# The partition sums of the late adaLN vectors issued one gate block later

## The chip, the cores and the metric

The kernel runs on one core of a Trainium2 chip. The metric is device time in microseconds (us) of one execution, lower is better. The core has five engines with instruction queues of their own: TensorE (PE, its weight loads are shown as PEld), VectorE (DVE), ScalarE (ACT), GpSimd (POOL) and SyncE (SP), which here only issues DMAs. Each queue is worked off in the order in which the program put it.

## What is computed

A decoder layer for one sequence of 1024 rows and 1024 columns. A conditioning vector `c` gives six vectors of 1024 numbers each; two of them scale and shift the input before the first half, two do so before the second, and two are gates on what the halves add:

```python
mod = jax.nn.silu(c) @ w_ada[l] + b_ada[l]
shift1, scale1, gate1, shift2, scale2, gate2 = [m[:, None, :] for m in jnp.split(mod, 6, axis=-1)]
h = layer_norm(x) * (1.0 + scale1) + shift1
z = h @ w_in[l]                       # columns for attention, S5 and two merge gates
...
mix = (jax.nn.sigmoid(g_a) * y_a + jax.nn.sigmoid(g_b) * y_b) @ w_o[l]
x = layer_norm(alpha * x + gate1 * mix) * ln1_g[l] + ln1_b[l]
h2 = layer_norm(x) * (1.0 + scale2) + shift2
...
x = layer_norm(alpha * x + gate2 * ff) * ln2_g[l] + ln2_b[l]
```

`y_a` is attention with three branches over `z`, `y_b` a linear recurrence (S5) with a gated linear unit, and `ff` a gated MLP with a convolution of width 3.

## The kernel before, in words

Products are made in pieces: an operand is split into a high and a low part, and three matmuls (lines 131 to 133, `mm3`) of 128x512 make one product. A product of 128 output columns with all 1024 rows (`gemmT`) is 48 such matmuls, in two halves of 24.

After `h` is made, sixteen **gate blocks** `z_gate(0)` to `z_gate(15)` compute the merge gates, 128 columns each; below they are called z0 to z15. They are followed by **jobs**: `r0` and `r1` (the raw keys and values for the compressed branch, tile `kc`), then keys, queries and the rest. z0 to r1 are 18 blocks whose order on TensorE, VectorE, ScalarE and GpSimd is that of the program text (`manual_schedule`); later parts are ordered by a scheduler.

One gate block does this, in the order of the text: fetch its split weights and split those of the next block (ScalarE line 112 makes the high part `wh`, VectorE or GpSimd line 113 the low part `wl`; both have two buffers, so the split waits until TensorE has finished the block before); pass the last block's product through a tanh (`z_out`, line 825); two **late steps** in z4 to z15; a piece of the S5 work (`s5_block`), with a second piece between the two halves of the product; and the product itself, tile `zm`.

The S5 work goes in four groups. On TensorE a group is `s5pk`, `s5pu` (lines 644, 650), then `s5pw` (669, transposes of `s5W`, which GpSimd makes), then `s5pb` (690), and at last `s5py` (748, 750), which needs the tile `s5X` that VectorE finishes at lines 731 and 732 after products and scans (704 to 725).

The late steps build the four vectors scale2 (v = 4), shift2 (3), gate1 (2) and gate2 (5). Each needs eight steps `late(v, k)`: a slab of 128x1024 of `w_ada` is multiplied by one column of silu(c) and added to an accumulator `acc` on VectorE (line 270 for the first, 272 for the others). Two steps go with each gate block, so v = 4 is complete in z7, v = 3 in z11 and v = 2 in z15. The eighth step is followed at once by the **sum over the 128 partitions** on TensorE:

- for v = 4 and 3, `ada_cols` (line 263): eight matmuls of a 128x128 piece of `acc` with a column of ones into the tile `adac` (the profile shows 16 records), and VectorE adds the bias (line 264, tile `mod`);
- for v = 2 and 5, two matmuls with the ones as the weights (line 801, tile `grow`, four records), VectorE adds them to a row `brow` that SP loaded (lines 798 and 802), and SP stores the row in DRAM (line 803, `gr_d`).

v = 5 has its eight steps one by one in the eight turns of the loop over `d` after attention. The weight slabs arrive in a ring `wr` of three buffers, loaded by SP (line 89).

Of the kernel before, what the change touches and what calls it, by code (L numbers as in the profile page):

```python
# [33 lines left out]
def kernel(  # L34
# [13 lines left out]
    def ap(t, off, *dims):  # L48
        return bass.AP(tensor=t.tensor, offset=t.offset + off, ap=[list(d) for d in dims])
# [4 lines left out]
    def Bt(shape, dt=F32, name="b"):  # L54
        return sp.tile(shape, dt, name=name, tag="B", bufs=20)
# [7 lines left out]
    def ps(shape=(P, 512), name="ps"):  # L63
        return pp.tile(list(shape), F32, name=name, tag="ps", bufs=4)
# [195 lines left out]
    def ada_cols(v, acc, k0=0, nk=KD):  # L260
        p = ps(name="adac")
        for k in range(nk):
            TE.matmul(p[:, k:k + 1], acc[:, P * k:P * k + P], ones[:, 0:1], start=True, stop=True)
        V.scalar_tensor_tensor(mod[:, MOD[v], k0:k0 + nk], p[:, 0:nk], 1.0 if v in (1, 4) else 0.0,
                               modb[:, 8 + 8 * v + k0:8 + 8 * v + k0 + nk], op0=OP.add, op1=OP.add)
# [495 lines left out]
    def s5_block(budget):  # L761

        debt[0] = max(debt[0] - budget, -budget)
        while debt[0] < 0:
            t = next(s5, 0)
            if t == 0:
                break
            if t is None:
                debt[0] = 0.0
                break  # L770
            debt[0] += t
        block[0] += 1
# [13 lines left out]
    def late(v, k, hold={}):  # L786
        if k == 0:
            hold[v] = Bt([P, 1024], name="acc")
        ada_acc(hold[v], late_i[v, k], k)
        if k < KD - 1:  # L790
            return
        acc = hold.pop(v)
        if v in (3, 4):
            ada_cols(v, acc)
            return
        gi = 0 if v == 2 else 1
        br = Bt([1, 1024], name="brow")
        SP.dma_start(br, ap(b_ada, v * D, [0, 1], [1, D]))
        for h in range(2):
            p = ps(name="grow")  # L800
            TE.matmul(p[0:1], ones[:, 0:1], acc[:, 512 * h:512 * h + 512], start=True, stop=True)
            V.tensor_add(br[:, 512 * h:512 * h + 512], br[:, 512 * h:512 * h + 512], p[0:1])
        SP.dma_start(gr_d[gi:gi + 1], br)

    sgs = {}

    def z_gate(m):
        wh, wl = W.get(zm_i[m])
        if m:
            z_out(m - 1)  # L810
        late_steps("z", m)
        s5_block(S5_US)
        sgs[m] = mm("zm")
        gemmT(sgs[m], wh, wl, hH, hL, KD)
# [3 lines left out]
    def late_steps(kind, n):  # L818
        for _ in range(n_late(kind, n)):
            late(*lateada[late_n[0]])  # L820
            late_n[0] += 1

    def z_out(m):
        sg = Bt([P, 1024], name="sg")
        A.activation(sg, sgs.pop(m), AF.Tanh, scale=0.5)
        A.dma_start(zm_d[m], sg)
# [149 lines left out]
    with tc.manual_schedule(engines={V.engine, A.engine, G.engine, TE.engine}):  # L976
        for kind, n in ORDER[:N_HAND]:
            if kind != "z":
                if n == 0 and kind == "r":
                    z_out(15)  # L980
                s5_block(S5_US)
            jobs[kind](n)
            if kind != "z":
                late_steps(kind, n)
    assert next(s5, 0) == 0
    S5 = uc = None
    for kind, n in ORDER[N_HAND:-1]:
# [225 lines left out]
    def load_sg(d):  # L1213
        if d < KD:
            ga, gb = Bt([P, 1024], name="ga"), Bt([P, 1024], name="gb")
            SP.dma_start(ga, zm_d[d])
            SP.dma_start(gb, zm_d[8 + d])
            sgs[d] = (ga, gb)
# [12 lines left out]
    for d in range(KD):  # L1231
        ga, gb = sgs.pop(d)
        wa = W.get(p3_i[d][0])
        pz = mm("z1")
        gemmT(pz, wa[0][:, 1], wa[1][:, 1], lambda k: yT[k][0], lambda k: yT[k][1], 4)
        pa = mm("ya")
        gemmT(pa, wa[0][:, 0], wa[1][:, 0], lambda k: oT[k][0], lambda k: oT[k][1], 4)
        wb = W.get(p3_i[d][1])
        late(5, d)
        load_sg(d + 1)  # L1240
        V.scalar_tensor_tensor(ga, ga, 1.0, pa, op0=OP.add, op1=OP.mult)
        s2 = Ct([P, 1024], name="s2")
        for h in range(2):
            c0 = slice(512 * h, 512 * h + 512)
            pg = ps(name="zg2")
            for k in range(4):
                mm3(pg, wb[0][:, k], wb[1][:, k], yT[k][0][:, c0], yT[k][1][:, c0], k == 0, k == 3)
            A.activation(s2[:, c0], pg, AF.Tanh, scale=0.5)
            V.scalar_tensor_tensor(s2[:, c0], s2[:, c0], 1.0, pz[:, c0], op0=OP.add, op1=OP.mult)
            V.scalar_tensor_tensor(s2[:, c0], gb[:, c0], 1.0, s2[:, c0], op0=OP.add, op1=OP.mult)  # L1250
            V.scalar_tensor_tensor(mixF[h][:, d], s2[:, c0], 0.5, ga[:, c0], op0=OP.mult, op1=OP.add)
        if 2 <= d < 6:
            wo.append(W.get(wo_i[d - 2]))
        if d == 5:
            split_mix(0, (0,))
# [538 lines left out]
```

## Time and profile before

| what | us |
|---|---|
| median of 3 runs | 1666.48 |
| lowest and highest of them | 1665.79, 1666.56 |
| the profiled execution, its own time | 1662.42 |
| its span, first to last instruction | 1660.7 |
| TensorE busy in the span | 1559.5 (94%) |
| VectorE busy | 1246.9 (75%) |
| ScalarE busy | 687.6 (41%) |
| GpSimd busy | 664.9 (40%) |

The span is 1.72 us shorter than the execution's own time, which has the start and the end around it. The profiled execution is 4.06 us under the median of the runs. A busy share says how long an engine had instructions in work, not who held up whom. For that there are the chain that ended last, the list of waits, and the timeline with the idle time in front of each instruction in square brackets and, behind the arrow, what ended it. [...]

### The profile page before, as it was taken

The numbers are of one execution on the slowest core, as the hardware profiler recorded it, in microseconds if no ns is written. First come the engines' busy times: TensorE is split into PE (matmuls) and PEld (weight loads), VectorE is DVE, ScalarE is ACT, GpSimd is POOL, SyncE is SP. The second block draws the span as 40 slices with busy tenths as digits, with TensorE's granted clock in tenths as the row PEclk, the third lists the DMA queues.
The fourth block names the chain that finished last, engine by engine and source line by source line (L and its number), as shares of the span: only waits on it lengthen the run. The fifth ranks groups of instructions, "written<-read, shape, count | busy, mean of one in ns | idle before, by whom it ended". The sixth has DMA issues, their size and how long they took to land.

```text
span 1660.7 us, 21550 instructions
## 1 busy us (share of the span) xinstructions
PE 1559.5 (94%) x7707; PEld 1304.5 (79%) x7707; DVE 1246.9 (75%) x2302; ACT 687.6 (41%) x1309; POOL 664.9 (40%) x559
## 2 busy tenths in 40 slices
PE   7999899899999999999999677999999998899996
PEld 4888788688989999778787455888888886688885
DVE  8698687555399999756686878888888887855448
ACT  4324323234399999512313633444444343311101
POOL 5345434000066566222425014555555555532006
PEclk8999899999999999999999798999999999999998
DMA  9334555422200010454511112222222237422102
GB/s 342 78 90 123 166 173 168 131 77 81 60 20 1 14 39 2 143 170 146 174 55 64 63 29 86 87 91 77 76 77 89 77 110 267 168 102 102 38 11 92
DMA packets 150129, 164.36 MB, mean 99 GB/s; under 512 B 20633, under 2 KB 123777, under 8 KB 150021
## 3 DMA queue, kind: packets, MB, share of 16 engines
q1 hardware_dynamic: 146357, 151.74, 28.7%
q10 hardware_dynamic: 3664, 11.24, 2.0%
q8 instruction: 61, 1.00, 0.3%
q14 instruction: 47, 0.39, 0.1%
HBM read 132.04 MB, written 30.91 MB: 98 GB/s over the span
## 4 chain that ended last, share of the span: by engine, by line
PE 73%; DVE 16%; ACT 5%; issue 3%; DMA 2%; SPq 0%; POOL 0%; DVEq 0%; ACTq 0%
PE up L1462 4%; PE up L1463 4%; PE up L1464 4%; PE dn L1610 4%; PE dn L1612 4%; PE dn L1611 4%; PE oacc L1096 3%; PE zm L131 3%; PE zm L132 3%; PE zm L133 3%; PE upX L1462 2%; PE pT L1107 2%; PE upX L1463 2%; PE upX L1464 2%; ACT Pm L1066 2%
## 5 line engine op out<-in xcount | busy, mean ns | idle before, releaser
L1070 POOL TENSOR_SCALAR Pm<-Pm,gate,fc 128x64 f32<-128x64 f32 (+4 forms) x192 | 124.3, 664 | 56.8 <-DVE fc L1068 56.2
L112 ACT ACTIVATE wh<-wr 128x1024 fp32r<-128x1024 f32 (+3 forms) x59 | 57.7, 978 | 184.6 <-PE zm L132 64.0
L1610 PE MATMUL dn<-dnh,fh 128*128 128x512 f32 x320 | 124.6, 389 | 0.9 <-DVE facc L1759 0.9
L1759 DVE SCALAR_TENSOR_TENSOR facc<-facc,dn 128x512 f32<-128x512 f32 x96 | 64.5, 682 | 80.2 <-PE dn L1612 80.0
L1611 PE MATMUL dn<-dnl,fh 128*128 128x512 f32 x320 | 124.5, 389 | 0.0
L1612 PE MATMUL dn<-dnh,fl 128*128 128x512 f32 x320 | 124.5, 389 | 0.0
L1066 ACT ACTIVATE Pm<-Pm,ng 128x64 f32<-128x64 f32 (+6 forms) x192 | 114.6, 602 | 6.4 <-DVE ng L1047 5.0
L111 POOL TENSOR_TENSOR wr<-wr,g2b 128x1024 f32<-128x1024 f32 x22 | 65.1, 2973 | 118.1 <-DMA wr<-in_w_down_dram 101.9
L1530 POOL TENSOR_TENSOR cv<-cv 128x1024 f32<-128x1024 f32 x22 | 62.1, 2825 | 118.1 <-ACT cv L1529 118.1
L1111 DVE TENSOR_TENSOR Pt<-pT,Pt 128x512 fp32r<-128x512 f32 (+1 forms) x160 | 100.6, 643 | 9.7 <-ACT Pt L1110 8.2
L1096 PE MATMUL oacc<-Pt,Vs 128*128 128x256 f32 x528 | 102.7, 304 | 0.9 <-DVE Pt L1111 0.4
L131 PE MATMUL zm<-hTh,wh 128*128 128x512 f32 x256 | 101.5, 397 | 0.4 <-ACT uc L582 0.4
L133 PE MATMUL zm<-hTh,wl 128*128 128x512 f32 x256 | 100.0, 391 | 1.5 <-DVE wl L113 1.5
L1391 POOL TENSOR_TENSOR ul<-wr,uh 128x512 fp32r<-128x512 f32 x40 | 69.6, 1761 | 76.1 <-ACT uh L1390 76.1
L132 PE MATMUL zm<-hTl,wh 128*128 128x512 f32 x256 | 100.1, 391 | 0.0
L1107 PE MATMUL pT<-ident,Pm 128*128 128x128 f32 x592 | 91.3, 273 | 1.9 <-DVE yl L1170 1.0
L1110 ACT ACTIVATE Pt<-pT 128x512 fp32r<-128x512 f32 (+1 forms) x160 | 87.4, 560 | 13.0 <-PE pT L1107 11.8
L113 DVE TENSOR_TENSOR wl<-wr,wh 128x1024 fp32r<-128x1024 f32 (+2 forms) x40 | 54.5, 1363 | 45.4 <-ACT wh L112 45.3
L113 POOL TENSOR_TENSOR wl<-wr,wh 128x1024 fp32r<-128x1024 f32 (+1 forms) x19 | 40.8, 2148 | 114.2 <-ACT wh L112 112.2
L1462 PE MATMUL up<-h2b,uh 128*128 128x512 f32 (+1 forms) x184 | 72.2, 392 | 14.4 <-DVE bias L1475 11.6
L1489 DVE SCALAR_TENSOR_TENSOR cv<-up,cw,cv 128x511 f32<-128x511 f32 x88 | 65.6, 745 | 20.7 <-ACT cv L1484 19.1
L1096 PEld LDWEIGHTS oacc<-Pt,Vs 128*128 128x128 f32 x528 | 75.5, 190 | 5.4 <-DVE Pt L1111 3.1
(487 smaller groups left out, 4817.6 us busy)
## 6 DMA issues: line engine op xcount, KB each, us to landing
wr<-in_w_up_dram SPq DMA_DIRECT2D x44, 512.0 KB, 4.7
wr<-in_w_in_dram SPq DMA_DIRECT2D x32, 512.0 KB, 5.9
wr<-in_w_ada_dram SPq DMA_DIRECT2D x32, 512.0 KB, 4.4
ff_d<-cv SPq DMA_DIRECT2D x22, 512.0 KB, 2.6
wr<-in_w_down_dram SPq DMA_DIRECT2D x22, 512.0 KB, 3.5
fl<-ff_d SPq DMA_DIRECT2D x22, 512.0 KB, 6.6
ar<-in_w_ada_dram SPq DMA_DIRECT2D x16, 512.0 KB, 9.8
zm_d<-sg ACTq DMA_DIRECT2D x16, 512.0 KB, 3.8
```

Of the source, the lines that this page charges most:

```text
L131: TE.matmul(po, wh, rh, start=start, stop=False, skip_group_check=skip)
L132: TE.matmul(po, wh, rl, start=False, stop=False, skip_group_check=skip)
L133: TE.matmul(po, wl, rh, start=False, stop=stop, skip_group_check=skip)
L1066: A.activation(Pm[ii][:, c0:c0 + n], Pm[ii][:, c0:c0 + n], AF.Exp, bias=ng[:, ii, br:br + 1], scale=-1.0, accum_out=dn[:, ii, br:br + 1])
L1070: G.tensor_scalar(Pm[ii][:, c0:c0 + n], Pm[ii][:, c0:c0 + n], gate[:, i, 3 * h + br:3 * h + br + 1], fc[:, ii, br:br + 1], op0=OP.mult, op ...
L1096: TE.matmul(acc[:, a0:a0 + 256], vt, ptile[:, hl, 256 * w:256 * w + 256], start=(first and n == 1), stop=(last and n == nmm), skip_group_c ...
L1107: TE.transpose(p[:, o:o + P], Pm[e][:, c0:c0 + P], ident)
L1111: V.tensor_sub(pt[:, 1, 0:wt], p[:, 0:wt], pt[:, 0, 0:wt].bitcast(F32))
L1462: TE.matmul(po, wh[:, q], h, start=(q == 0 and j not in (3, 4, 7)), stop=False, skip_group_check=True)
L1610: TE.matmul(p, ff[0][:, c0], wd[0][:, s], start=(e == 0), stop=False)
L1611: TE.matmul(p, ff[0][:, c0], wd[1][:, s], start=False, stop=False)
L1612: TE.matmul(p, ff[1][:, c0], wd[0][:, s], start=False, stop=(e == len(fs) - 1))
```

## The change

The eighth step now only puts the finished accumulator on a list (`late_sum`). A new function `late_sums` makes the sums of what is on the list, with the same instructions as before. It is called in three places: in each gate block after `z_out` and before that block's own late steps; in r0 after `z_out(15)`; and in the loop over `d`, in its last turn, right after the step, which is where the sum of v = 5 was before. A call of `late_steps` for jobs that have no late steps is dropped.

```diff
         ada_acc(hold[v], late_i[v, k], k)
         if k < KD - 1:
             return
-        acc = hold.pop(v)
-        if v in (3, 4):
-            ada_cols(v, acc)
-            return
-        gi = 0 if v == 2 else 1
-        br = Bt([1, 1024], name="brow")
-        SP.dma_start(br, ap(b_ada, v * D, [0, 1], [1, D]))
-        for h in range(2):
-            p = ps(name="grow")
-            TE.matmul(p[0:1], ones[:, 0:1], acc[:, 512 * h:512 * h + 512], start=True, stop=True)
-            V.tensor_add(br[:, 512 * h:512 * h + 512], br[:, 512 * h:512 * h + 512], p[0:1])
-        SP.dma_start(gr_d[gi:gi + 1], br)
+        late_sum.append((v, hold.pop(v)))
+
+    late_sum = []
+
+    def late_sums():
+
+        while late_sum:
+            v, acc = late_sum.pop()
+            if v in (3, 4):
+                ada_cols(v, acc)
+                continue
...
@@ z_gate
         if m:
             z_out(m - 1)
+        late_sums()
         late_steps("z", m)
         s5_block(S5_US)
@@ the loop over the 18 blocks
                 if n == 0 and kind == "r":
                     z_out(15)
+                    late_sums()
                 s5_block(S5_US)
             jobs[kind](n)
-            if kind != "z":
-                late_steps(kind, n)
@@ the loop over d after attention
         late(5, d)
+        if d == KD - 1:
+            late_sums()
```

What left out lines in `late_sums` do is the removed block from `gi =` on, word for word.

How this moves instructions is shown at three places. First TensorE between z6 and z7 (the first `zm` triple is the end of z6, the second the start of z7), before:

```order
L131 MATMUL zm<-hTh,wh 128x512
L132 MATMUL zm<-hTl,wh 128x512
L133 MATMUL zm<-hTh,wl 128x512
L263 MATMUL adac<-ones,acc 128x1 x8
L669 MATMUL s5pw<-ident,s5W 128x2x64 x8
L131 MATMUL zm<-hTh,wh 128x512
```

With the change the same place, between z6 and z7:

```order
L131 MATMUL zm<-hTh,wh 128x512
L132 MATMUL zm<-hTl,wh 128x512
L133 MATMUL zm<-hTh,wl 128x512
L669 MATMUL s5pw<-ident,s5W 128x2x64 x8
L131 MATMUL zm<-hTh,wh 128x512
```

The `adac` matmuls of v = 4 now stand 48 `zm` matmuls and one `s5pb` group later, between z7 and z8; those of v = 3 move in the same way from the head of z11 to that of z12.

Second, TensorE between z14 and z15 before:

```order
L132 MATMUL zm<-hTl,wh 128x512
L133 MATMUL zm<-hTh,wl 128x512
L801 MATMUL grow<-acc,ones 1x512 x2
L131 MATMUL zm<-hTh,wh 128x512
L132 MATMUL zm<-hTl,wh 128x512
```

and with the change between z15 and r0 (line 801 is now 808):

```order
L132 MATMUL zm<-hTl,wh 128x512
L133 MATMUL zm<-hTh,wl 128x512
L808 MATMUL grow<-acc,ones 1x512 x2
L131 MATMUL kc<-hTh,wh 128x512
L132 MATMUL kc<-hTl,wh 128x512
```

z15 now follows z14 with nothing between, and the `grow` matmuls stand ahead of r0's product `kc`.

Third, VectorE at z7 and z8. Before, the addition of line 264 stood right behind the eighth step:

```order
L272 SCALAR_TENSOR_TENSOR acc<-wr,scol,acc 128x1024 x2
L264 SCALAR_TENSOR_TENSOR mod<-adac,modb 128x8
L704 TENSOR_TENSOR s5r_1761<-s5B,s5E 128x4x127
L705 TENSOR_TENSOR s5r_1761<-s5B,s5E 128x4x127
L706 TENSOR_TENSOR s5r_1761<-s5r_1761 128x4x127
```

and with the change it stands in z8:

```order
L709 TENSOR_TENSOR s5r_1752<-s5B,s5E 128x4x127
L710 TENSOR_TENSOR s5r_1752<-s5r_1752 128x4x127
L113 TENSOR_TENSOR wl<-wr,wh 128x1024
L264 SCALAR_TENSOR_TENSOR mod<-adac,modb 128x8
L270 TENSOR_SCALAR acc<-wr,scol 128x1024
L272 SCALAR_TENSOR_TENSOR acc<-wr,scol,acc 128x1024
```

It has moved behind six S5 products and the weight split of z8, and ahead of the first late step of v = 3. In the same way the two additions of line 802 (now 809) move from in front of the last S5 group's scans to behind its lines 721 to 725, and SP's load and store of the row (798 and 803, now 805 and 810) move behind three weight loads and one load of `per`. ScalarE and GpSimd keep their order.

## Rows read from the trace of the kernel before

**Rows 1.** The page, TensorE's busy time, and the shares of the chain by engine.

```profile
PE 1559.5 (94%) x7707; PEld 1304.5 (79%) x7707; DVE 1246.9 (75%) x2302; ACT 687.6 (41%) x1309; POOL 664.9 (40%) x559
...
PE 73%; DVE 16%; ACT 5%; issue 3%; DMA 2%; SPq 0%; POOL 0%; DVEq 0%; ACTq 0%
```

**Rows 2.** Waits of PE from 150 to 345 us: total us, times, longest.

```profile
PE adac L263 <- DVE acc L272: 7.0, 1, 7.0
PE grow L801 <- DVE acc L272: 4.8, 1, 4.8
```

**Rows 3.** Timeline of PE, end of z6 to z7: start us, us, instruction [idle before].

```profile
189.15 0.39 PE L133 MATMUL zm<-hTh,wl 128*128 128x512 f32 x1
196.57 3.54 PE L263 MATMUL adac<-ones,acc 128*128 128x1 f32 x16 [7.03 <-DVE acc L272]
199.97 1.95 PE L669 MATMUL s5pw<-ident,s5W 128*128 128x128 f32 x8
201.57 0.78 PE L131 MATMUL zm<-hTh,wh 128*128 128x512 f32 x1
```

**Rows 4.** Timeline, first matmul of z8.

```profile
215.42 0.39 PE L131 MATMUL zm<-hTh,wh 128*128 128x512 f32 x1
```

**Rows 5.** Timeline of DVE in z7.

```profile
190.44 1.99 DVE L113 TENSOR_TENSOR wl<-wr,wh 128x1024 fp32r<-128x1024 f32 x1 [0.23 <-ACT wh L112]
192.35 4.07 DVE L272 SCALAR_TENSOR_TENSOR acc<-wr,scol,acc 128x1024 f32<-128x1024 f32 x2
```

**Rows 6.** Timeline: the s5W that z7's s5pw reads, and z7's wl.

```profile
147.08 1.35 POOL L618 TENSOR_TENSOR s5W<-s5W,s5tA 128x512 f32<-128x512 f32 x1
...
173.46 1.23 DVE L113 TENSOR_TENSOR wl<-wr,wh 128x1024 fp32r<-128x1024 f32 x1 [0.54 <-ACT wh L112]
```

**Rows 7.** Timeline of PE, end of z13 to z14.

```profile
297.46 0.40 PE L133 MATMUL zm<-hTh,wl 128*128 128x512 f32 x1
297.69 1.03 PE L669 MATMUL s5pw<-ident,s5W 128*128 128x128 f32 x8
298.49 0.47 PE L131 MATMUL zm<-hTh,wh 128*128 128x512 f32 x1
```

**Rows 8.** Timeline of PE, end of z14 to z15.

```profile
311.05 0.39 PE L133 MATMUL zm<-hTh,wl 128*128 128x512 f32 x1
316.27 3.45 PE L801 MATMUL grow<-acc,ones 128*1 128x512 f32 x4 [4.84 <-DVE acc L272]
319.65 0.57 PE L131 MATMUL zm<-hTh,wh 128*128 128x512 f32 x1
```

**Rows 9.** Timeline of PE and DVE, end of z10 to z11.

```profile
254.99 0.39 PE L133 MATMUL zm<-hTh,wl 128*128 128x512 f32 x1
255.22 1.84 PE L263 MATMUL adac<-ones,acc 128*128 128x1 f32 x16
256.92 0.36 PE L690 MATMUL s5pb<-s5U,s5Wx 128*128 128x128 f32 x1
257.09 0.17 DVE L264 SCALAR_TENSOR_TENSOR mod<-adac,modb 128x8 f32<-128x8 f32 x1 [3.23 <-PE adac L263]
```

**Rows 10.** Timeline, first matmul of r0.

```profile
330.76 0.39 PE L131 MATMUL kc<-hTh,wh 128*128 128x512 f32 x1
```

**Rows 11.** Timeline of PE at the sum of v = 5, after attention.

```profile
802.15 0.39 PE L133 MATMUL zg<-yh,wl 128*128 128x512 f32 x1
802.47 1.88 PE L801 MATMUL grow<-acc,ones 128*1 128x512 f32 x4
804.28 0.50 PE L131 MATMUL z<-yh,wh 128*128 128x512 f32 x1
```

**Rows 12.** Windows: us, busy (x) of PE, PEld, DVE, ACT, POOL; PEclk, DMA share, GB/s.

```profile
196.50:200.10 3.60, 3.53 (x17) 3.56 (x18) 0.00 (x0) 0.00 (x0) 3.52 (x4) 0.50 0.80 236
225.00:245.00 20.00, 20.00 (x118) 17.63 (x117) 19.30 (x42) 6.60 (x14) 9.28 (x6) 1.00 0.61 192
```

**Rows 13.** Timeline in z9 and z10: the last instruction on s5X, its reader.

```profile
231.25 0.68 DVE L732 TENSOR_TENSOR s5X<-s5r 64x508 f32<-64x508 f32 x1
...
237.18 0.38 PE L748 MATMUL s5py<-s5T,s5U 128*128 128x128 f32 x2
```

**Rows 14.** Timeline of SP and ACT: a weight load in r0, and its split.

```profile
334.79 0.38 SPq L89 DMA_DIRECT2D wr<-in_w_in_dram  x1
...
367.82 1.06 ACT L112 ACTIVATE wh<-wr 128x1024 fp32r<-128x1024 f32 x1 [3.91 <-issue]
```

More of the change, by code (lines that the diff above doesn't have):

```diff
@@ L791, in late @@
             return
-        acc = hold.pop(v)
-        if v in (3, 4):
-            ada_cols(v, acc)
-            return
-        gi = 0 if v == 2 else 1
-        br = Bt([1, 1024], name="brow")
-        SP.dma_start(br, ap(b_ada, v * D, [0, 1], [1, D]))
-        for h in range(2):
-            p = ps(name="grow")
-            TE.matmul(p[0:1], ones[:, 0:1], acc[:, 512 * h:512 * h + 512], start=True, stop=True)
-            V.tensor_add(br[:, 512 * h:512 * h + 512], br[:, 512 * h:512 * h + 512], p[0:1])
-        SP.dma_start(gr_d[gi:gi + 1], br)
+        late_sum.append((v, hold.pop(v)))
[6 more added lines that the diff above has]
+                continue
+            gi = 0 if v == 2 else 1
+            br = Bt([1, 1024], name="brow")
+            SP.dma_start(br, ap(b_ada, v * D, [0, 1], [1, D]))
+            for h in range(2):
+                p = ps(name="grow")
+                TE.matmul(p[0:1], ones[:, 0:1], acc[:, 512 * h:512 * h + 512], start=True, stop=True)
+                V.tensor_add(br[:, 512 * h:512 * h + 512], br[:, 512 * h:512 * h + 512], p[0:1])
+            SP.dma_start(gr_d[gi:gi + 1], br)
     sgs = {}
```

## The prediction

> **What bounds the kernel now.** I read the page first. TensorE is busy for 94% of the span and holds 73% of the chain that ended last; VectorE holds 16% [rows 1]. So time is mostly TensorE's own work, and a change that does no less work can only win where TensorE stands still. The second view is the list of TensorE's waits between 150 and 345 us, the stretch from z4 to r0: it has two entries in all, 7.0 us in front of `adac` and 4.8 us in front of `grow`, both ended by VectorE's accumulation [rows 2]. The third is the timeline around the two. At the head of z7 TensorE is done with z6 and idles 7.03 us, because the sums stand next in its queue and the accumulator is not finished [rows 3]; VectorE cannot begin the split of line 113 before z6 is over, and the two late steps follow it, 4.07 us that end at 196.42 [rows 5]. The head of z15 repeats this, with 4.84 us idle in front of `grow` [rows 8]. At the head of z11 the accumulator is ready in time: `adac` follows the last product without a gap [rows 9].
>
> The idle time is not all that is lost. In the stretch of z7's sums the granted clock was 0.50, which is the lower of TensorE's two levels [rows 12]; the `adac` records take 3.54 us there and 1.84 us in z11, the eight `s5pw` transposes 1.95 us there and 1.03 us in z14 [rows 3, 7, 9]. I therefore count from matmul to matmul and not by the waits.
>
> **Part 1: v = 4, from z7 to z8.** Before, the time from the last matmul of z6 (189.15) to the first of z8 (215.42) is 26.27 us [rows 3, 4]. With the change it has three pieces.
> - From z6 to z7 only `s5pw` is left. z14 has just this head: 297.46 to 298.49, 1.03 us [rows 7].
> - z7 itself: z14, which like z7 has an `s5pb` group between its halves, runs from 298.49 to its last matmul at 311.05, and one matmul step of 0.23 us (297.46 to 297.69) is added: 12.79 us [rows 7, 8].
> - The moved sums at z8: in z11 they put 255.22 to 256.92, that is 1.70 us, into the queue [rows 9].
>
> Together 15.52 us, so the gain is 26.27 - 15.52 = 10.75 us. What could replace the old wait has been ready for long: the `s5W` that `s5pw` reads was written by 148.43 and the split weights of z7 by 174.69 [rows 6]. The price of the moved sums lies between nothing (if z8 has an idle place that the trace of before doesn't show) and 3.54 us, the record at the lower clock [rows 3]. I take z11's because TensorE comes to z8 out of an unbroken gate, as it does there.
>
> **Part 2: v = 3, from z11 to z12.** The sums cost 1.70 us where they are and 1.70 us where they go, both in an unbroken run of products. Zero, within 1.84 us on either side (the bare record of rows 9).
>
> **Part 3: v = 2, from z15 to r0.** Before, the last matmul of z14 (311.05) to the first of r0 (330.76) is 19.71 us [rows 8, 10]. With the change z15 follows z14 after 0.23 us and takes its 11.11 us (319.65 to 330.76) [rows 8, 10]. Then come the `grow` matmuls ahead of r0. They cost 1.90 us in the loop after attention, where TensorE comes to them from full work: 802.15 to 804.28, less one step of 0.23 [rows 11]. Sum 13.24 us, gain 6.47 us. The upper bound of `grow` is 3.38 us, its cost behind the wait (316.27 to 319.65) [rows 8], the lower one nothing; I take the row behind full work.
>
> **Part 4: v = 5.** Its sum stays where it was. Zero.
>
> **What else is moved.** Line 264 now stands on VectorE behind z8's weight split, which itself cannot start before z7's last matmul. At z7 that split started 1.29 us after z6's last matmul (189.15 to 190.44), and it takes 1.23 us where nothing disturbs it, as at 173.46 [rows 3, 5, 6]: 2.52 us, and the sums need 0.23 + 1.70 = 1.93. So the addition finds them done. In z12 and r0 VectorE may come to its addition before TensorE has ended the gate, and then it stands still with all that is behind it. [...] That slack is 5.25 us in z9 and z10: `s5X` was finished at 231.93 and its reader started at 237.18 [rows 13]. I cost the holds at nothing, since they should be shorter than this; if they aren't, the rest lands on TensorE in front of `s5py`.
>
> On SP the store of the row now waits behind r0's `grow`, some 2 us after z15's end, with the weight loads behind it. The first of them was issued at 334.79 and its tile was split at 367.82, 33.03 us later [rows 14], so a hold of a few us is covered. The accumulators live one gate longer, which shifts the rotation of the 20 shared buffers; the rows give it no price, and I leave it to the range.
>
> **The sum.** 10.75 + 0 + 6.47 + 0 = 17.2 us. Against the profiled execution, 1662.42 - 17.2 = 1645.2 us. That execution is 4.06 us under the median of 1666.48, and the gain is a difference inside the program, so I take it from the median: **1649.3 us**. The parts behind r0 do the same work in almost the same order, and the chain there is TensorE's, so I expect the shift to last to the end.
>
> **The rivals.**
>
> *Part 1 fails: z7's wait only changes its owner* (6%). `s5pw` or z7's own product then waits for something that the idle time had hidden, up to where TensorE stood before. For it: every other engine gets 10.75 us less. Against it: the two inputs of rows 6, and the list of waits, which has no other entry. Only part 3 is left: 1666.48 - 6.47 = 1660.0 us.
>
> *Part 3 fails: r0 or r1 takes the gain back* (5%). SP's queue stops at the row's store, and the next jobs' weights come late. For it: three DMA kinds stand behind that store. Against it: the 33.03 us of rows 14. Only part 1 is left: 1655.7 us.
>
> *The shift does not reach the end* (4%). A later stage waits for something that does not depend on TensorE's time, such as a transfer, and 17.2 us vanish there. For it: 6% of the span TensorE is not busy. Against it: DMA holds 2% of the chain [rows 1]. Then 1666.5 us, no change.
>
> *VectorE becomes the bound, and the kernel is slower* (3%). The place is the three additions in z8, z12 and r0. If VectorE reaches each of them at the start of the preceding gate, it stands still for a whole gate, 11.11 us. In z8 and z12 the slack of 5.25 us is taken off: 2 x 5.86 = 11.72 us; in r0, the last S5 group, I grant none: 11.11 us. Sum 22.8 us, 5.6 more than the gain: 1672.1 us. It decides from holds that put more than 17.2 us on TensorE. For it: VectorE was busy for 19.30 of 20 us from 225 to 245 us [rows 12], so it has little to give there. Against it: in z8 the addition stands behind a split that waits for the same gate to end.
>
> **How the numbers follow.** The forecast has the rest, 82%. Its own range: with both sums at their dear end the gain is 17.2 - 1.84 - 1.48 = 13.9 us; with the sums at z8 free 18.9 us, and with r0's too 20.8. The difference of 4.06 us between one execution and the median is put on both sides: 1641.6 to 1656.6. Both ends together are unlikely, so I give **1643.5 to 1656.5 us**; this takes in the second rival at 1655.7, and leaves out the others with 13% and the far ends. A difference of 0.2%, 3.3 us, is about what a measurement of this kernel can tell from none. Faster by more than that: the forecast and the first two rivals, 93%. Within it: the third, 4%. Slower: the fourth, 3%.
>
> **What would show it.** In the profile of the changed kernel the list of waits from 150 to 345 us should have neither `adac` nor `grow` behind the accumulation. z7's first matmul should come about 1.0 us after z6's last, with the clock granted in full; z8 should start some 15.5 us after z6's end, with about 1.7 us of `adac` in front of it; z15 should follow z14 at once; and r0 should start some 13.2 us after z14's end. The lead over the trace of before should be 10.75 us at z8 and 17.2 us at r0, and still be there at the end. The forecast is wrong if a new wait stands in front of `s5pw`, `s5py` or r0's product, if VectorE idles for more than 5 us in front of lines 264 or 809, or if the lead shrinks after r0.

## The result and the profile after

The changed kernel takes 1646.8 us in the median of 4 runs (1641.96 to 1650.65) against 1666.5 (1665.79 to 1667.07) before: ratio 0.9884, 95% interval 0.9858 to 0.991. Forecast were 1649.3 us, in a range from 1643.5 to 1656.5. A second comparison of the same kernel (run `again`, below) gives 1649.0 us and 0.9897 (0.9883 to 0.9911). One run of a kernel below, of `fill`, took 6628 us, which no profile explains, and its ratio leaves it out.

The page of the changed kernel, against [rows 1]: TensorE's busy time is 7.2 us less although it does the same matmuls, and the chain is TensorE's as before. The 7.2 us are no measure of the change: in the profile of `again` TensorE is busy for 1561.8 us, more than before.

```profile
PE 1552.3 (95%) x7707; PEld 1298.0 (79%) x7707; DVE 1254.7 (76%) x2302; ACT 687.1 (42%) x1309; POOL 661.6 (40%) x559
...
PE 73%; DVE 17%; ACT 5%; issue 3%; DMA 2%; POOL 0%; SPq 0%; DVEq 0%; ACTq 0%
```

The list of TensorE's waits from 150 to 345 us, which had two entries [rows 2], is empty now. The timeline of PE (start us, us, instruction, in brackets the idle time before it and what ended it) shows the end of z6, z7 and the head of z8, answering to [rows 3, 4]; then the end of z15 and the head of r0, answering to [rows 8, 10].

```profile
187.57 0.40 PE L133 MATMUL zm<-hTh,wl 128*128 128x512 f32 x1
187.80 1.03 PE L669 MATMUL s5pw<-ident,s5W 128*128 128x128 f32 x8
188.59 0.47 PE L131 MATMUL zm<-hTh,wh 128*128 128x512 f32 x1
...
201.16 0.39 PE L133 MATMUL zm<-hTh,wl 128*128 128x512 f32 x1
201.38 1.84 PE L263 MATMUL adac<-ones,acc 128*128 128x1 f32 x16
203.08 0.49 PE L131 MATMUL zm<-hTh,wh 128*128 128x512 f32 x1
...
309.80 0.39 PE L133 MATMUL zm<-hTh,wl 128*128 128x512 f32 x1
310.11 1.88 PE L808 MATMUL grow<-acc,ones 128*1 128x512 f32 x4
311.92 0.50 PE L131 MATMUL kc<-hTh,wh 128*128 128x512 f32 x1
```

z7 follows z6 after 1.02 us (187.57 to 188.59), and z8 starts 15.51 us after z6's last matmul (26.27 before). From the end of z7 to r0 no row has idle time in front of TensorE. The windows (us, then the busy time with the count of PE, PEld, DVE, ACT and POOL, the granted clock as a share of full speed, the DMA share, GB/s) say that the clock was 1.00 through both places; [rows 12] had 0.50 there. These are the two levels that the trace of before shows: of 56 windows of half a microsecond from 186 to 214 us, 54 have 1.00 or 0.50, and the two in which it changes 0.55 and 0.71.

```profile
187.50:203.10 15.60, 15.60 (x92) 13.56 (x90) 12.27 (x11) 10.59 (x26) 11.96 (x8) 1.00 0.58 167
...
309.80:313.30 3.50, 3.50 (x12) 1.39 (x11) 1.95 (x3) 2.08 (x2) 0.00 (x0) 1.00 0.36 145
```

VectorE's timeline at the moved additions: in z8 it finds the sum done, in z12 it stands still for 1.76 us, in r0 for 2.25. SP's timeline in r0: the store of the row goes out at 312.73, the weight load behind it 4 us later.

```profile
203.94 0.16 DVE L264 SCALAR_TENSOR_TENSOR mod<-adac,modb 128x8 f32<-128x8 f32 x1
...
257.58 0.17 DVE L264 SCALAR_TENSOR_TENSOR mod<-adac,modb 128x8 f32<-128x8 f32 x1 [1.76 <-PE adac L263]
257.66 2.13 DVE L270 TENSOR_SCALAR acc<-wr,scol 128x1024 f32<-128x1024 f32 x1
...
311.17 0.68 DVE L809 TENSOR_TENSOR brow<-brow,grow 1x512 f32<-1x512 f32 x1 [2.25 <-PE grow L808]
...
312.73 0.24 SPq L810 DMA_DIRECT2D gr_d<-brow  x1
316.71 0.39 SPq L89 DMA_DIRECT2D wr<-in_w_in_dram  x1
```

### The profile page after: what moved, and what is told of

Same layout as the page of the kernel before. It is cut to its first block, busy times and chain, and to the rows that moved or that the text cites. A ratio compares the mean times of both kernels' runs of the same rounds, so it can differ in the third digit from the quotient of the medians.

```text
span 1640.2 us, 21545 instructions
## 1 busy us (share of the span) xinstructions
PE 1552.3 (95%) x7707; PEld 1298.0 (79%) x7707; DVE 1254.7 (76%) x2302; ACT 687.1 (42%) x1309; POOL 661.6 (40%) x559
## 4 chain that ended last, share of the span: by engine, by line
PE 73%; DVE 17%; ACT 5%; issue 3%; DMA 2%; POOL 0%; SPq 0%; DVEq 0%; ACTq 0%
PE up L1471 4%; PE up L1473 4%; PE up L1472 4%; PE dn L1619 4%; PE dn L1621 4%; PE dn L1620 4%; PE zm L131 3%; PE zm L133 3%; PE zm L132 3%; PE oacc L1103 3%; PE upX L1471 2%; PE pT L1114 2%; PE upX L1472 2%; PE upX L1473 2%; ACT Pm L1073 2%
## 5 line engine op out<-in xcount | busy, mean ns | idle before, releaser
L1117 ACT ACTIVATE Pt<-pT 128x512 fp32r<-128x512 f32 (+1 forms) x160 | 87.3, 560 | 13.2 <-PE pT L1114 12.2
L113 DVE TENSOR_TENSOR wl<-wr,wh 128x1024 fp32r<-128x1024 f32 (+2 forms) x40 | 58.5, 1462 | 39.4 <-ACT wh L112 39.2
L1471 PE MATMUL up<-h2b,uh 128*128 128x512 f32 (+1 forms) x184 | 72.2, 392 | 14.4 <-DVE bias L1484 11.6
```

Source lines behind the costliest of these rows:

```text
L1471: TE.matmul(po, wh[:, q], h, start=(q == 0 and j not in (3, 4, 7)), stop=False, skip_group_check=True)
```

## The experiments

Whole runs of this kernel differ by some us, whichever kernel it is (eleven runs of the kernel before spread from 1662.96 to 1669.24), and a good part of that lies outside the changed stretch. Where z6 ends alone differs from 187.57 to 190.24 us between the profiles. So the best measure of a mechanism here is one stretch of the trace: **from z6's last matmul to r0's first**, which holds all moved sums but the one of v = 5. Before it is 141.61 us (189.15 to 330.76) [rows 3, 10], in the changed kernel 124.35 (187.57 to 311.92): 17.26 us less. The table has it for every kernel, beside the ratio of whole runs. One per cent is 16.7 us.

| kernel | stretch, us | less than before | ratio of runs, 95% interval |
|---|---|---|---|
| the change | 124.35 | 17.26 | 0.9884 (0.9858 to 0.991) |
| again | 124.35 | 17.26 | 0.9897 (0.9883 to 0.9911) |
| cols_only | 131.03 | 10.58 | 0.9936 (0.9921 to 0.995) |
| row_only | 135.21 | 6.40 | 0.996 (0.9945 to 0.9976) |
| steps_first | 135.30 | 6.31 | 0.9958 (0.9945 to 0.9972) |
| half | 127.61 | 14.00 | 0.9911 (0.9898 to 0.9925) |
| late_add | 124.35 | 17.26 | 0.9904 (0.9889 to 0.992) |
| fill | 136.54 | 5.07 | 0.9984 (0.9971 to 0.9996) |
| double | 132.83 | 8.78 | 0.9963 (0.995 to 0.9975) |
| double_apart | 128.05 | 13.56 | 0.9934 (0.9915 to 0.9952) |
| v5_jobs | 124.35 | 17.26 | 0.9871 (0.9857 to 0.9884) |
| v5_shift | 124.36 | 17.25 | 0.9886 (0.9869 to 0.9903) |
| v5_defer | 124.35 | 17.26 | 0.9865 (0.9846 to 0.9884) |

Theory A is the prediction's: the gain is the time that TensorE stands still for a sum whose accumulator is not ready, and the lower clock behind that (0.50 in [rows 12]); the sums' own cost only moves.

### The same kernel again

No edit.

> The changed kernel once more, for its spread. Theory A (the gain is the two idle waits and the lower clock behind them, 17.2 us): median 1646 to 1650.5 us, 16 to 20 us under the kernel before; in the profile the lead over the kernel before is 17.2 us at r0, up to 1.6 more where z2's wait falls out shorter, and what comes on top later differs from run to run by 2 to 4 us, with the head of the loop over d. Rival B (the new life of the accumulators also speeds up the loop over d): the lead grows by over 2 us in that loop every time, and the median is at or under 1645.

Median 1649.0 us, 17.8 under the kernel before in the same comparison. Its stretch is the changed kernel's to the hundredth. What the first comparison had on top of the stretch does not come with the change: there z6 had ended 1.58 us earlier than before (187.57 against 189.15), here it ended 0.86 us later (190.01). The other surplus lay in the loop over `d` after attention, where TensorE waits for the weight split of line 113. The lists of TensorE's waits from 690 to 800 us (total us, times, longest), first of the changed kernel's first profile, then of this one:

```profile
PE z L133 <- DVE wl L113: 1.7, 2, 1.1
```

```profile
PE z L133 <- DVE wl L113: 1.9, 1, 1.9
PE z L131 <- ACT wh L112: 0.5, 1, 0.5
```

And the windows from 720 to 760 us, of the kernel before, the change and `again`: clock 0.96, 1.00 and 0.92.

```profile
720.00:760.00 40.00, 38.05 (x160) 30.67 (x159) 23.42 (x26) 7.23 (x10) 8.63 (x4) 0.96 0.55 179
```

```profile
720.00:760.00 40.00, 39.45 (x175) 32.34 (x174) 22.89 (x22) 7.34 (x10) 7.64 (x4) 1.00 0.60 195
```

```profile
720.00:760.00 40.00, 40.00 (x164) 32.52 (x165) 23.64 (x26) 7.33 (x10) 8.38 (x5) 0.92 0.53 169
```

From the last `oacc` matmul to the first `wo`, which holds most of this loop, the three take 134.13, 131.73 and 135.71 us. So this stage varies by 4 us with the same program, rival B falls, and the first comparison was a little lucky.

### One kind of sum at a time

`cols_only` makes the row sum of v = 2 at once; `row_only` has the same two lines with `if v in (3, 4):` and makes the column sums at once.

```diff
         late_sum.append((v, hold.pop(v)))
+        if v == 2:
+            late_sums()
```

> Only the column sums of v = 4 and v = 3 are moved; the row sum of v = 2 stays at the head of z15. Theory A: lead at z8 10.75 us (up to 1.6 more from z2), at r0 the same, the wait in front of the row sum is 4.8 us as before, and the median is 1666.5 - 10.75 = 1655.8 us. Rival C (one backlog of VectorE stands behind both waits, so that what z7 no longer waits is waited at z15): the wait in front of the row sum grows to 10 us or more, and the median is over 1661.

> Only the row sum of v = 2 is moved, from z15 to r0; the column sums stay at the heads of z7 and z11. Theory A: no lead at z8 beyond what z2 gives, 6.5 us gained between z14's end and r0's first matmul, median 1666.5 - 6.47 = 1660.0 us. Rival C (one backlog for both waits): z15's wait was a rest of z7's, and r0 gains what is left, under 3 us: over 1663. Rival D (the store of the row on SP gives the gain back in r0 or r1): lead of 6.5 at r0, under 2 at the end.

Medians 1654.7 and 1659.3 us. The stretches add up: 10.58 + 6.40 = 16.98 of 17.26. In `row_only` the time from z14's end to r0 falls by 6.71 us, as with the whole change; from z6's end to z8 it takes 26.58 us instead of 26.27, with a wait that is longer by 0.5. Each kernel's list of waits from 150 to 345 us has only the wait that was left in (4.8 as before; 7.5 against 7.0):

```profile
PE grow L810 <- DVE acc L272: 4.8, 1, 4.8
```

```profile
PE adac L263 <- DVE acc L272: 7.5, 1, 7.5
```

Rival C, one backlog behind both waits, falls, since the row sum's wait did not grow. Rival D falls too: in the profile of `row_only` the lead is 6.45 us at r0 and 6.27 at the first matmul of the keys (`kT`), so r0 and r1 do not take it back. At the end of that profile only 1.98 us are left; the rest is lost in the loop over `d` and between the first `up` and the first `dn` matmul, stages that vary from profile to profile (below). Whole runs are 0.4% shorter, which is the 6.4 us.

### The accumulator earlier instead of the sum later

In the kernel before, each gate block's late steps go ahead of the next block's weight split on VectorE; the sums stay where they were. `first` (its definition is left out) covers the weights from z4 to r0.

```diff
-        r = W.get(idx)
+        r = (W.split(idx + 1), W.load(idx + 3), W.hl.pop(idx))[2] if idx in first else W.get(idx)
...
-        wh, wl = W.get(zm_i[m])
-        if m:
-            z_out(m - 1)
+        wh, wl = W.get(zm_i[m], split=1) if n_late("z", m) else W.get(zm_i[m])
         late_steps("z", m)
+        W.split((zm_i[m + 1] if m < 15 else kc_i[0]) + 1)
+        if m: z_out(m - 1)
```

> The sums stay where they were before; instead VectorE makes the two late steps ahead of the weight split of the next block (z4 to z8 and z15), so the accumulator is ready earlier by about that split. Theory A: the wait at z7 falls from 7.03 to about 4.8 us (less the 1.99 of the split and the 0.23 in front of it), the one at z15 from 4.84 to about 2.9 (less 0.79 and 1.14), so the median is 1666.5 - 4.1 = 1662.4 us, a little less where the clock falls later. Rival C: the waits only change owner (the weights of z8 or r0 come late instead), 1666. Rival E (the split is not what held the accumulator back, the transfer of its slab is): both waits unchanged, 1666.

Median 1659.8 us, and more gained than I had counted: the waits fall to 3.0 and 2.8 us.

```profile
PE adac L263 <- DVE acc L272: 3.0, 1, 3.0
PE grow L801 <- DVE acc L272: 2.8, 1, 2.8
```

VectorE's timeline in z7 tells why the first is shorter than the 4.8 expected: the steps start at 188.62, while z6's last matmul comes only at 189.60. I had let them start after z6's end, as the split does that has to wait for it [rows 5]. The idea holds (what stands ahead of the accumulator on VectorE sets the wait), and moving the split is worth somewhat over a third of moving the sum.

```profile
188.62 4.20 DVE L272 SCALAR_TENSOR_TENSOR acc<-wr,scol,acc 128x1024 f32<-128x1024 f32 x2
```

### Half a gate later instead of a whole one

The call of `late_sums` moves between the two halves of the product; the one in r0 goes (left out here).

```diff
             if h:
+                late_sums()
                 s5_block(S5_US)
...
-        late_sums()
         late_steps("z", m)
```

> The sums stand only half a gate later than before the change: between the two halves of z7, z11 and z15. In the changed kernel z7's first half ended about 5.6 us after z7's start (188.59), so at 194.2, and the accumulator was ready at 194.85. Theory A (only the time by which the sum comes too early is lost): a wait of 0.5 to 1.5 us in front of the column sum in z7, none in z15, lead at r0 16 to 17.2 us as in the changed kernel less that wait, median 16 to 18.5 us under the kernel before. Rival B (a whole gate of distance is needed, because VectorE is behind by more than the steps): waits of over 3 us in z7 or z15, lead at r0 under 13. Rival F (VectorE's additions in the middle of the S5 products hold it up): the waits are short, but s5py or the product of r0 waits for VectorE by over 2 us.

The wait is as expected, 1.26 us in z7 and none in z15. Its price is not: z8 starts 18.75 us after z6's end, 3.24 later than in the changed kernel. The timeline of PE and the windows of z7:

```profile
196.75 1.92 PE L263 MATMUL adac<-ones,acc 128*128 128x1 f32 x16 [1.26 <-DVE acc L272]
198.53 2.81 PE L690 MATMUL s5pb<-s5U,s5Wx 128*128 128x128 f32 x16
200.99 0.77 PE L131 MATMUL zm<-hTh,wh 128*128 128x512 f32 x1
```

```profile
197.00:201.00 4.00, 4.00 (x32) 4.00 (x32) 0.17 (x1) 0.01 (x1) 3.92 (x4) 0.82 0.88 252
201.00:205.00 4.00, 4.00 (x16) 3.22 (x15) 2.13 (x4) 2.36 (x4) 0.11 (x1) 0.75 0.33 68
```

Behind the wait and the sums the clock fell: 4 us at 0.82 and 4 at 0.75 are 0.72 + 1.00 = 1.72 us of full-speed work lost, with the wait 2.98 of the 3.24. So the change's whole gate of distance was worth 3.2 us more than half a gate, though the wait that half a gate leaves is small. In part for this reason the median, 14.6 us under the kernel before, misses the 16 to 18.5 that I had expected.

### VectorE's additions later

The matmuls of the sums stay where the change put them. `late_sums` only lists its additions and the row's store; `late_adds` issues them, behind the late steps and the next S5 piece.

```diff
         late_sums()
         late_steps("z", m)
         s5_block(S5_US)
+        late_adds()
```

> The sums stay on TensorE where the change put them, but VectorE's additions behind them come later: in z8 and z12 behind part of the next S5 piece, in r0 behind all of the S5 piece (and with them SP's store of the row, some 7 us later). In the changed kernel VectorE stands still 1.76 us in z12 and 2.25 us in r0 in front of them; in this one it should not stand still there. Theory A (those holds cost nothing, and SP's store has time): lead at r0 and at kT as in the changed kernel within 0.3 us, median 17 to 18.7 us under the kernel before. Rival D (SP's store holds back weights): r1's or k0's product waits for its weights, median under 15 us below before. Rival F (VectorE's holds cost): the lead grows by 1 to 4 us at r0 or behind it.

The stretch is 124.35 us, the same as with VectorE's holds, and from r0's first matmul to the first of `kT` both kernels take 26.19 us. VectorE no longer stands still in front of the additions: in z12 the first late step of v = 2, which the addition had held, starts 1.63 us ahead of z12's first matmul (258.60), in the changed kernel 0.26 us behind it (257.40).

```profile
256.97 0.73 DVE L271 TENSOR_SCALAR acc<-wr,scol 128x1024 f32<-128x1024 f32 x1
```

So those holds cost TensorE nothing. The place of the store stays untested: here it goes out at 314.17, 1.05 us behind r0's first matmul, in the changed kernel 0.81 behind it, so that the run moved VectorE's work but hardly SP's. My expectation of 7 us for the store was wrong. The median, 1651.6 us, is 15.0 us under the kernel before and misses the 17 to 18.7 expected; it lies next to the number of rival D, but no product waits for its weights up to `kT`. Over its whole profile the granted clock was 0.973, near the 0.974 of `again` and under the 0.978 of the changed kernel's first profile, and the stage between `up` and `dn` took 480.8 us (476.4 and 478.1 in the two profiles of the changed kernel).

### Idle time filled with useless products

The kernel before, with 28 matmuls ahead of the sum in z7 and 18 ahead of that in z15 that write a tile nobody reads.

```diff
+        fill({4: 28, 2: 18}.get(v, 0))
...
+        p = ps(name="fill")
+        for i in range(n):
+            TE.matmul(p, cur[0][:, i % 8], hH(i % 8)[:, 0:512], start=True, stop=True)
```

> The kernel before, with the sums where they were, but TensorE makes products that nobody reads while it would wait: 28 matmuls of 128x512 ahead of the column sum in z7 (6.4 us at full clock) and 18 ahead of the row sum in z15 (4.1 us). It parts the idle time from the lower clock behind it: the accumulators come no earlier, but TensorE does not stand still for long. Theory A (of the gain of 10.75 in z7 7.0 are waiting and 3.7 the lower clock; of the 6.5 in z15 4.8 and 1.7): left waits under 1.2 us, the sums at 1.84 and 1.88 us, z8's start 3.6 us earlier after z6's end than in the kernel before, r0's 1.7 after z14's, median 5.3 us under the kernel before, though it does more work. Rival K (the clock falls by the kind of matmul, the sums' one column or row, and not by the standing still): sums at 3.5 us as before, no gain or some loss, median within 1.5 us of before.

The left waits are 0.68 and 0.76 us, and the sums take 1.92 and 1.88 us, against 3.54 and 3.45 before [rows 3, 8], so rival K falls for one sum behind full work:

```profile
195.60 1.92 PE L263 MATMUL adac<-ones,acc 128*128 128x1 f32 x16 [0.68 <-DVE acc L272]
197.38 1.07 PE L669 MATMUL s5pw<-ident,s5W 128*128 128x128 f32 x8
198.21 0.47 PE L131 MATMUL zm<-hTh,wh 128*128 128x512 f32 x1
...
311.88 1.88 PE L811 MATMUL grow<-acc,ones 128*1 128x512 f32 x4 [0.76 <-DVE acc L272]
```

The stretch is 5.07 us shorter, as expected (5.3), with 46 matmuls more. From z6's end (188.18) to z8's first matmul (211.02) it takes 22.84 us, 3.43 less than before: of part 1's 10.76 us a third is the clock and the rest waiting. In part 3 a quarter is: from z14's end to r0 it takes 18.08 us, 1.63 of 6.71 less. Of whole runs the gain is only 2.7 us (0.7 to 4.8), less than the 5.3 expected and than the stretch shows; that number alone would not rule out rival K, which had up to 1.5. The profile points at the time between the first `up` and the first `dn` matmul: 481.2 us, against 476.4 in the profile of the kernel before. But this stage takes from 476.4 to 482.1 us in the thirteen profiles whose edit leaves it alone, and what sets it is open.

### The sums twice

`double` makes each sum twice in a row; `double_apart` makes the column sums again one gate later.

```diff
-        for k in range(nk):
+        for k in list(range(nk)) * 2:
...
                 TE.matmul(p[0:1], ones[:, 0:1], acc[:, 512 * h:512 * h + 512], start=True, stop=True)
+                TE.matmul(p[0:1], ones[:, 0:1], acc[:, 512 * h:512 * h + 512], start=True, stop=True)
```

```diff
                 ada_cols(v, acc)
+                again.append((v, acc))
...
+        for v, acc in again:
+            ada_cols(v, acc)
+        again.clear()
         late_sums()
```

> Every sum is issued twice in a row, column sums and row sums, the second over the first. It prices what the moved sums cost where they now stand. Theory A: z8's and z12's head become 1.70 us longer each, r0's 1.9 us and the turn d = 7 of the loop after attention 1.9 us: 7.2 us in all, median 10.6 us under the kernel before instead of 17.8; lead at z8 9.05 instead of 10.75 and at r0 11.9 instead of 17.2. Rival G (the sums are hidden where they now stand, in idle places of TensorE that the moved order opened, and the gain is larger than the waits for that reason): under 3 us more, lead at r0 over 15.

> The changed kernel with the column sums of v = 4 and v = 3 made twice, but the second time one gate later (z8 and z9, z12 and z13) instead of right behind the first. With two in a row, 3.49 us of one-column matmuls without a pause, the clock was granted at 0.50 for 3.4 us behind them, and z8 to z10 took 1.59 us more. Theory L (so long an unbroken row of one-column matmuls counts for the clock as standing still does, and one sum alone is too short for that): no fall of the clock in z8, z9, z12 and z13, each extra sum costs 1.70 us, lead at r0 3.4 us less than in the changed kernel, median 14.4 us under before. Rival M (the fall came from what the sum does to the products behind it, whenever it is repeated): falls of 3.4 us there too, lead at r0 5 to 7 us less, median under 12.8.

The second sums cost what the first do: z8's head grows by 1.79 us, z12's by 1.78, r0's by 1.72. So the sums are not hidden (rival G falls), and the terms 1.70 and 1.90 of the prediction are near the price. But `double` loses 8.48 us against the changed kernel in the stretch, 3.2 more than these. They are lost in the products behind the doubled column sums, where nothing waits: z8 to z10 takes 41.30 us instead of 39.71, z12 to z14 43.12 instead of 41.52. The timeline and windows of `double` in z8 show the clock fall about 1 us behind the doubled sums:

```profile
203.14 3.62 PE L263 MATMUL adac<-ones,acc 128*128 128x1 f32 x32
206.63 0.49 PE L131 MATMUL zm<-hTh,wh 128*128 128x512 f32 x1
...
207.66 0.55 PE L132 MATMUL zm<-hTl,wh 128*128 128x512 f32 x1
208.00 0.63 PE L133 MATMUL zm<-hTh,wl 128*128 128x512 f32 x1
208.43 0.63 PE L131 MATMUL zm<-hTh,wh 128*128 128x512 f32 x1
```

```profile
206.00:210.00 4.00, 4.00 (x17) 3.34 (x18) 3.16 (x7) 0.00 (x0) 0.00 (x0) 0.72 0.91 289
210.00:214.00 4.00, 4.00 (x16) 3.23 (x16) 4.00 (x11) 0.00 (x0) 0.00 (x0) 0.86 0.79 253
```

Of 4 us at 0.72 and 4 at 0.86 the loss is 1.12 + 0.56 = 1.68 us, against 41.30 - 39.71 = 1.59. In z12 the clock falls in the same way (0.84 from 263 to 267 us, 0.73 from 267 to 271). In `double_apart` the windows behind the first and the second sum of v = 4 have 1.00, and so have those of v = 3 (260 to 268 and 273 to 277 us):

```profile
204.00:208.00 4.00, 4.00 (x19) 3.32 (x20) 3.96 (x8) 0.45 (x1) 0.00 (x0) 1.00 0.75 215
217.00:221.00 4.00, 4.00 (x18) 3.27 (x18) 3.96 (x4) 0.04 (x1) 1.59 (x1) 1.00 0.44 150
```

Its stretch is 3.70 us longer than the changed kernel's, 1.85 for each extra sum. Theory L holds in the stretch, and rival M's falls are not there: the clock fell behind both rows of one-column matmuls of 3.5 us and behind none of 1.7. The doubled row sums in r0, eight records of 512 columns in 3.52 us, were not followed by a fall (322.00 to 326.00 at 1.00). The medians miss what was expected: `double` is 6.2 us under the kernel before instead of 10.6, `double_apart` 9.5 instead of 14.4, which by itself would suit rival M. For `double` the falls explain most of it (3.2 us); for `double_apart` the stretch has 13.56 us, and in its profile the stage between `up` and `dn`, which the edit does not touch, is the longest of all (482.1 us).

### The next wait: the loop over d

`v5_jobs` takes the steps of v = 5 out of the loop after attention and puts one each behind k0, c0, k1, c1 and q0 to q3; `v5_shift` uses c0, k1, c1, q0, q1, q2, n0 and q3; `v5_defer` also makes the sum only after the loop over the row blocks that makes `wo`.

```diff
-    n_late = lambda kind, n: 2 if kind == "z" and n >= 4 else 0
+    n_late = lambda kind, n: 2 if kind == "z" and n >= 4 else int(kind in "kqc")
...
-        late_i[5, d] = W.add([(None, ada_src(5, d))], [1024], raw_only="late")
...
-        late(5, d)
-        if d == KD - 1:
-            late_sums()
...
         late_steps(kind, n)
-    assert late_n[0] == 24
+    late_sums()
+    assert late_n[0] == 32
```

> The changed kernel, and beside that the eight steps of v = 5 leave the loop over d after attention and go one by one into the jobs k0, c0, k1, c1 and q0 to q3, its sum behind q3. There VectorE was busy for 15 to 20 of 30 us and the transfers took a quarter of the time; in the loop over d the weight split waits for the transfers, TensorE waits 1.1 to 3.4 us for it, and from a wait of about 1.9 us on the granted clock falls behind it. Theory H (the loop's transfers are what it waits for): the wait and the fall go, the loop is 2 to 6 us shorter than in the other copy of the changed kernel, median 20 to 24 us under the kernel before. Rival I (the wait there is for the slabs of w_o and the split behind the product, not for the slabs of v = 5): the loop is as long as before within 1 us, median 17 to 18.7 us under before. Rival J (the jobs have no room: the weights or the accumulator's buffer come late): new waits between 345 and 460 us, under 16.

> As the kernel that moved the steps of v = 5 into the jobs, but the steps go into c0, k1, c1, q0, q1, q2, n0 and q3, so that the two ahead of the second keys, where TensorE waited 1.0 us for its weight split, are spread out. Theory H: that wait goes or falls under 0.5, the loop after attention stays without waits of over 0.5 us, median 22 to 23 us under the kernel before. Rival J (the jobs have too little room wherever the steps stand): another wait of 1 us or more between 345 and 460 us, median 20.5 to 22.

> As the run with the steps of v = 5 in c0 to q3, and its sum comes only in the stage before the second half, among the transposes h2p, where TensorE waited 3.7 and 0.8 us for ScalarE. Theory H with the sum hidden in that wait: 1.9 us less than with the sum behind q3, median 23.5 to 25 us under the kernel before. Rival N (the accumulator's buffer, held from c0 to there, holds back what wants to be put in it, in attention or in the loop after it): new waits of TensorE between 440 and 830 us of over 2 us, median less than 21 us under before.

Medians 1645.0, 1646.8 and 1643.4 us. In all three the wait of the loop is gone, and from the last `oacc` to the first `wo` they take 127.36 us, 127.36 and 127.37, against 131.73 and 135.71 in the two profiles of the changed kernel (1.9 of this is the sum that has left the loop). The window of `v5_jobs` from 720 to 760 us:

```profile
720.00:760.00 40.00, 40.00 (x178) 33.15 (x177) 15.46 (x18) 8.30 (x11) 8.68 (x5) 1.00 0.43 143
```

So theory H holds for the loop in this: with the steps of v = 5 its wait goes. What the wait was for, the timeline of `again` shows in front of its longest one:

```profile
708.28 1.28 DVE L272 SCALAR_TENSOR_TENSOR acc<-wr,scol,acc 128x1024 f32<-128x1024 f32 x1 [0.68 <-DMA wr<-in_w_ada_dram]
709.59 0.33 SPq L89 DMA_DIRECT2D wr<-in_w_o_dram  x1
713.89 1.23 DVE L111 TENSOR_TENSOR wr<-wr,g1b 128x1024 f32<-128x1024 f32 x1 [4.33 <-DMA wr<-in_w_o_dram]
716.12 1.04 ACT L112 ACTIVATE wh<-wr 128x1024 fp32r<-128x1024 f32 x1
719.80 0.79 PE L133 MATMUL z<-yh,wl 128*128 128x512 f32 x1 [1.85 <-DVE wl L113]
```

The late step ends at 709.56, SP issues the load of the `w_o` slab at 709.59, VectorE waits 4.33 us for that slab, and the splits of `w_o` and of the next weights follow, for which TensorE waits. So the wait is for the slab of `w_o`, as rival I had it, and that slab is late because its load stands behind the step of v = 5. Whether the transfer of the slab of v = 5, its buffer in the ring or VectorE's step weighs most was not parted: the edit takes out all three.

The wait of 1.0 us in front of the second keys in `v5_jobs` is gone in `v5_shift`, whose median is nevertheless no better: 18.8 us under the kernel before, where 22 to 23 were expected. Its time between the first `up` and the first `dn` is 480.1 us, against 476.4 and 478.1 in the two profiles of the changed kernel; that is within what this stage varies by. `v5_defer` is 22.1 us under, where 23.5 to 25 were expected; TensorE has no wait of over 0.8 us between 440 and 830 us, so rival N falls. In `v5_defer` the sum sits among the transposes, but not for nothing: it takes 3.42 us, near the 3.45 that it took behind z15's wait [rows 8], where the granted clock was 0.53 (316.20 to 319.70 us), and not the 1.88 of [rows 11].

```profile
900.40 3.42 PE L807 MATMUL grow<-acc,ones 128*1 128x512 f32 x4 [0.80 <-ACT h2y L1306]
```

Against the kernel before, `v5_jobs` and `v5_defer` are faster by 1.3%; against the change their intervals touch those of its two comparisons, so that a gain of a few us over it is likely and not shown by the runs alone.

## Why the prediction was right

**Part 1** forecast 10.75 us from z6's end to z8's start; measured are 26.27 - 15.51 = 10.76. The three pieces hold one by one: head of z7 1.02 (1.03), sums 1.70 (1.70), z7 itself 12.79 (12.79). Counting from matmul to matmul was the step that mattered: the wait alone would have given 7.0, and `fill` shows that about a third is the clock (3.43 us). `cols_only` gives 10.58 for parts 1 and 2 together.

**Part 2** forecast zero. From z10's end to z12's start the time goes from 14.69 to 14.61 us, and the stretches around it become 0.14 and 0.15 longer: a loss of 0.2.

**Part 3** forecast 6.47 us, measured 19.71 - 13.00 = 6.71. The sum behind full work costs 1.81 us (310.11 to 311.92). The rest of the difference is that the 11.11 us which I took for z15 began behind a wait: the granted clock was 0.53 from 316.20 to 319.70 us and 0.98 from there to 323, and its first matmul took 0.57 [rows 8]; in the changed kernel they are 10.97 (299.14 to 310.11).

**Part 4** and the additions were costed at nothing. VectorE's holds are 0, 1.76 and 2.25 us, all under the 5 us that I had set as a limit, and `late_add` shows that they cost nothing. That what stands behind an addition waits with it was my assumption; in z12 it did. The first late step of v = 2 starts at 257.66, only behind the addition at 257.58 and 0.26 us behind z12's first matmul; in `late_add`, where the addition stands further back, it starts 1.63 us ahead of that matmul. z11 of the kernel before does not show it: the instruction behind the addition there started at 263.65 after 6.39 us of waiting for a DMA. The holds were shorter than the slack of 5.25 us between the end of `s5X` and its reader [rows 13]. That SP's store has time was argued from the 33.03 us, and no run put the store much later.

**The sum** was 17.2 us; the stretch gives 17.25 or 17.26 in five kernels that share this order on TensorE. That it agrees to 0.1 us is luck in part, since part 2 lost 0.2 and part 3 gained 0.24 more than forecast. The rivals fell: z7 has no new wait in front of `s5pw` or its product, r0 and r1 none behind SP's store, the lead is still there at the end (the last `dn` matmul comes 20.5 us earlier in the first profile and 12.2 in `again`, the medians say 19.7 and 17.8), and VectorE's idle time in front of the additions is not a gate long. By the profile of `again` alone the lead shrinks from 16.4 us at r0 to 12.2, which I had named as a sign of being wrong; 1.6 us of that lie in the loop over `d` and 1.7 between `up` and `dn`, and the profile of the kernel before, against which it is counted, is 4.06 us under its median.

**What I had not forecast** is the difference of 2.5 us between 1649.3 and the first median, 1646.8. `again` returns 1649.0. As far as the profiles show it is scatter: where z6 ends, whether the clock falls in the loop over `d` (1.00 and 0.92 from 720 to 760 us in the two profiles of the change), and the stage between `up` and `dn`.

## What to carry to other kernels

A small operation for whose input an engine stands still (7.03 and 4.84 us here) should be issued where its input has been ready for some time, and a whole block of distance cost nothing here, where the result is not needed soon: half a block left a wait of 1.26 us that cost 3.24. Price a wait of TensorE from matmul to matmul across it, since the lower clock behind it made nearly a third of the loss here (3.43 and 1.63 of 10.76 and 6.71 us). And measure such a change on the shortest stretch that holds it: that stretch agreed to 0.01 us between runs whose whole times differ by several.

## What the runs showed of the hardware

- The granted clock fell not only behind idle time. In `double` it fell twice behind 3.49 us of one-column matmuls without a pause (0.72 and 0.86 in the two windows of 4 us behind the first, 0.84 and 0.73 behind the second), and the 512-column products behind them took 1.59 and 1.60 us more. Behind 1.70 us of the same (`double_apart`), and behind 3.52 us of row sums with 512 columns (`double`), it did not fall: the windows have 1.00.
- Behind a short wait the clock fell in some runs and not in others. In the loop over `d` it fell behind a wait for the weight split of 1.86 us in the kernel before (0.50 from 737 to 739 us) and of 1.85 in `again` (0.92 from 720 to 760 us). Behind 1.86 us in `fill` and 1.76 in `double_apart` the steps between the next ten matmuls stayed at 0.22 to 0.24 us, where they were 0.42 and 0.43 in the kernel before from 737 to 739 us, and behind 1.10 us in the changed kernel the clock was 1.00; so the 1.9 us named ahead of `v5_jobs` are no boundary. In z7, 1.26 us of waiting with 1.92 us of column sums behind them were followed by a fall (`half`, 0.82 and 0.75), and 0.68 us with the same sums were not: the products behind them in `fill` came 0.23 us apart.
- With nothing to wait for, TensorE's time over 124 us repeated to 0.01 us in six profiles, on more than one chip.
